# Other instruction durations in the scheduler of a hybrid encoder trunk

## The chip, the cores and the metric

The program runs on one core of a Trainium2 chip. The metric is the device time of one execution in microseconds (us), the median of several runs; less is better. The core has a matrix engine (TensorE, in the rows PE, its weight loads PEld), a vector engine (VectorE, DVE), a scalar engine (ScalarE, ACT), GpSimd (POOL), and a queue (SyncE, SP) from which all transfers of this kernel are issued. Each engine takes its instructions strictly in the order in which the program was written; an instruction whose input isn't there holds up all that stand behind it on its engine.

## The reference

Two layers with shared weights run over two groups of tokens, 512 and 256, of width 1024. Everything is float32. Per layer:

```
h = rmsnorm(x) ; proj = h @ w_in            (q, k, v of four attentions A, B, C, D and 4 x 1024 gates)
o_A: neighbourhood attention with a bias    o_B: grouped-query attention, normed q and k, rotary
o_C: differential attention, ALiBi          o_D: sliding window with a sink, ALiBi
merged = sum over the branches of sigmoid(gate_b) * (o_b @ w_branch_b)
x += rmsnorm(merged @ w_out)
u = rmsnorm(x) @ w_up ; c = conv of width 3 over the tokens ; f = (gelu(gate) * val) @ w_down
x += rmsnorm(f)
```

## The kernel before

Features lie on the 128 partitions and the 768 tokens of both groups side by side on the free axis. Every operand of a product is split into two float32r parts h and l, and a product is made in three passes (h*h, h*l, l*h). So a block of 128 output features with a contraction over 1024 is 8 x 3 x 2 = 48 matmuls, 24 with 512 columns and 24 with 256.

What matters here is how the order of the instructions comes about. The program is written by about a dozen Python generators ("tasks"): the main line of a layer (projections, gates, output projection, feed-forward part), three attention `worker`s, loaders of bias tiles and branch outputs, tasks that empty PSUM, the norms. `Flow` keeps an estimated clock for each engine. Each helper that issues an instruction (`mm`, `tr`, `act`, `_dve` and those that call it, `rsqrt`, `dma`) adds that instruction's estimated duration to its engine's clock and returns the time at which the result may be used, 150 ns (`HOP`) after the estimated end. A task that needs a result says from which time on it can go on. `Flow.run` always resumes the ready task of the highest priority, where "now" is the estimated clock of TensorE; if none is ready, that clock is set forward to the next task's time, which is an estimated idle time of TensorE. Nothing of these times goes onto the chip: only the order of the instructions does.

The main line has the lowest priority, so its matmuls fill TensorE while an attention worker waits for ScalarE or VectorE. What it does meanwhile is a fixed list, `JOBS` (L58): the projections and, as `t`, 19 gate blocks made early (`EARLY`, L60), whose tanh is kept in DRAM. A unit of attention is one head for 256 queries (`unit`, L915): logits, bias and row maximum (L967, for B L949), exp, reciprocal (L994), scaling, transposes (L400), the split of the transposed probabilities, the product with the values, the sum of its two halves. There are 48 units a layer, in the order D, A, B, A, C; three run at a time.

After the last job the main line goes on with `gates` (L1204) for A, B, C, D in turn. Before its products for a branch it needs that branch's output back from DRAM, split (`o_load`, L1140): three times a buffer of the pool `P` (12 buffers, which the attention units also use), a transfer, a copy on ScalarE and a subtraction on VectorE. Then come the output projection and the feed-forward part. Each of the two ends with blocks that are made token group by token group (`grouped_tail`, L697), and as a group is done its norms are started (`sandwich` L637, `pre_norm` L579), while TensorE works on the next group.

All matrix products and the mean squares are issued at L396 in `mm`, transposes at L400, ScalarE's instructions at L412, VectorE's mostly at L426, L430 and L435.

Of the kernel before, what the change touches and what calls it, by code (L numbers as in the profile page):

```python
"""Hybrid gated encoder trunk on one core.

Activations are kept with features on partitions and the tokens of both request groups side by side on the
free axis (prompt 0..511, sample 512..767).  Every float32 operand x of a matrix product is split exactly into
h = float32r(x) and l = x - h, and a product is accumulated as h*h + h*l + l*h (attention logits also carry l*l).
"""
# [11 lines left out]
F32 = mybir.dt.float32  # L18
# [4 lines left out]
PSUM = bass.MemoryType.PSUM  # L23
# [3 lines left out]
KB = DM // 128  # L27
# [8 lines left out]
# the FFN's hidden blocks, in the parts that are on chip together  # L36
THIRDS = ((0, 7), (7, 14), (14, 22))
BR = "ABDC"
# the branches in the order of their gating
# [7 lines left out]
# columns of the per-layer parameter tile  # L47
P_N = 0            # four norm gains, KB columns each
P_GQ = 32          # gqa q gain, gqa q gain of the rotation partner, same for k
P_SUB = 36  # L50
P_LAM = 37         # q1, k1, q2, k2 (32 each), the same on every partition
P_SINK = 165       # four columns, the same on every partition
P_CONV = 169       # per up block: tap 0, tap 1, tap 2, bias
# [3 lines left out]
# What the tensor engine does while the attention runs: projections, and the products of early gates (t).  # L57
JOBS = "V D t A0 t t t VC B A1 t t t t t Cq0 t t Ck0 t t Cq1 Ck1 t t t t t t".split()  # L58
# the gates (branch, block) made early, in order
# [3 lines left out]
def unit_keys():  # L63
    """The weight units of a layer in the order of their use."""
# [26 lines left out]
def unit_data(key, w_in, w_branch, w_out, w_up, w_down):  # L91
    """The unit as [128, n]: contraction rows on partitions, then k block, then output column."""
# [39 lines left out]
def host_arrays(inputs, depth):  # L132
# [31 lines left out]
    # rpb laid out by (column, row offset, key column), NEG outside the column window  # L164
# [8 lines left out]
    # constants of the shapes  # L173
# [30 lines left out]
# blocks of w_out and of the last third of the FFN that are computed token group by token group  # L204
# [4 lines left out]
class Flow:  # L209
    """Emits the instructions of several tasks in an order that follows an estimate of the engines' times.  # L210

    A task is a generator that emits instructions and yields the time before which it has nothing to emit."""
# [34 lines left out]
class Slots:  # L247
    """The buffers of one tag: counts the live ones and knows when a free one may be written."""
# [6 lines left out]
    def ready(self):  # L255
        """The number of buffers that may be written now."""
        return sum(t <= self.flow.now for t in self.freed)
# [18 lines left out]
def both(*needs):  # L276
    """Waits until every one of the (slots, n) is free."""
    while any(s.ready() < n for s, n in needs):
        yield needs[0][0].flow.now + 100
# [21 lines left out]
class Pair:  # L301
    """Weights whose two parts lie in two buffers."""
# [13 lines left out]
class Part:  # L316
    """Weights in the columns of h whose tokens come to be known only after the weights' use."""
# [16 lines left out]
class Block:  # L334
    """A [128, 768] result in PSUM: in a double bank, or with another one in a double bank (their first 512
    columns) and a bank (the rest)."""
# [15 lines left out]
    def parts(self):  # L352
        """Its access patterns, with their columns."""
        if self.full is not None:
            return [(self.full, 0, T)]
        return [(self.half[0], 0, TP), (self.half[1], TP, T)]
# [6 lines left out]
def mixed(a, b):  # L363
    """The elements of a and b, each in its order, evenly mixed, a first."""
    key = [(i / len(x), n, e) for n, x in enumerate((a, b)) for i, e in enumerate(x)]
    return [e for _, _, e in sorted(key)]


class Trunk:
# [23 lines left out]
    def mm(self, out, lhsT, rhs, start, stop, *deps):  # L393
        n = out.shape[-1]
        ns = n * 0.4218 * (4 if lhsT.dtype == F32 else 1)
        self.nc.tensor.matmul(out=out, lhsT=lhsT, rhs=rhs, start=start, stop=stop)  # L396
        return self.f.on("pe", max(ns, 30), *deps)
# [12 lines left out]
    def act(self, out, in_, func, *deps, **k):  # L410
        n = self.size(out)
        self.nc.scalar.activation(out=out, in_=in_, func=func, **k)  # L412
        ns = n * 0.8336 + 80
# [8 lines left out]
    def _dve(self, out, *deps, rate=0.96, fixed=70):  # L422
# [6 lines left out]
    def stt(self, out, a, s, b, op0, op1, *deps):  # L429
        self.nc.vector.scalar_tensor_tensor(out=out, in0=a, scalar=s, in1=b, op0=op0, op1=op1)  # L430
        return self._dve(out, *deps, fixed=130)

    def ts(self, out, a, s1, s2, op0, op1, *deps):
# [4 lines left out]
        return self._dve(out, *deps, rate=1.92, fixed=70 if isinstance(s1, float) else 130)  # L438
# [73 lines left out]
    PASSES = ((0, 0), (0, 1), (1, 0))  # L512

    def mblock(self, out, w, rhs, nk, off=0, wait=None):
        """out: list of (PSUM AP, column range); w: unit; rhs(k, part, c0, c1): moving operand."""
# [16 lines left out]
    def bank(self):  # L532
        """A bank, of a double one or, if that leaves one for the norms, a single one."""
# [4 lines left out]
    def anyblock(self):  # L538
        """As dblock, but in two single banks if they are free sooner."""
# [14 lines left out]
    def rstd_bcast(self, b, n, t):  # L554
        """b: bank with the mean squares of n token tiles in columns 0, 2, ..; leaves 1/sqrt(mean + eps) on
        every partition, one column per token."""
# [10 lines left out]
    def mean_square(self, b, x, first, last, t):  # L567
        """Adds the mean over the partitions (and the middle axis) of x [128, j, 256], which holds squares."""
# [10 lines left out]
    def pre_norm(self, G, x, gain, h, last, first=False):  # L579
        """h = split(rmsnorm(x) * gain) for a group; x: four [128, 2, 256] APs, overwritten,  # L580
        with the times when they are there and when they may be written."""
# [55 lines left out]
    def sandwich(self, G, mix, msq, x_old, x_new, pre, h):  # L637
        """x_new = x_old + rmsnorm(mix) * gain; then h = split(rmsnorm(x_new) * pre) unless it is the end.
        mix comes multiplied by the gain, msq holds the squares without it."""
# [27 lines left out]
    def mix_evac(self, cols, blk, m, groups, mix, msq, gain, acc=None):  # L667
        """Brings an m block of mix (or of the last third of the FFN), times the gain of the norm to come, to
        SBUF and adds its squares."""
# [29 lines left out]
    def grouped_tail(self, tail, nk, key, rhs, wait, mix, msq, gain, sandwich, acc=None):  # L699
        """The first output blocks over all tokens, the others group by group, each group's norms started as it  # L700
        ends."""
# [38 lines left out]
    def v_tiles(self, name, units, tiles, vg):  # L740
        """Values of four heads, tokens on partitions: for each head h and l side by side."""
# [37 lines left out]
    def q_stack(self, src, scale, t0, users):  # L779
        """Two heads' queries, [h; l] for the first and [l; h] for the second."""  # L780
# [11 lines left out]
    def k_stack(self, src, t0, users):  # L792
        """Two heads' keys, for each the parts h and l on both halves of the partitions."""
# [11 lines left out]
    def head_stats(self, src, t):  # L805
        """1/rms over each half of the partitions of src [128, 768], as [128 tokens, 6 tiles, 2 halves]."""
# [12 lines left out]
    def bcast_mul(self, out, a, gain, s, tmp, *deps):  # L819
        """out = a * (1/rms of its half), rms given per token; tmp [128, 768] is overwritten."""  # L820
# [19 lines left out]
    def rope(self, blk, col, cs, key):  # L840
        """Rotated heads of a projection block, before (queries) or after (keys) the rms norm's division."""
# [24 lines left out]
    def c_stack(self, blk, scale, order, users):  # L866
        """32-wide sub-heads of two heads: for each head [128, 2, 768], the parts given by order on four
        quarters of the partitions."""
# [27 lines left out]
    UNITS = (0, 2, 1)  # prompt queries 0..255, sample, prompt queries 256..511  # L896
# [18 lines left out]
    def unit(self, name, h, u, q, k, v, bias, scales=None, oc=None):  # L915
        """Attention of one head for 256 queries (two tiles)."""
# [164 lines left out]
    def worker(self):  # L1081
        """Runs queued attention units, in order, as their operands become ready."""
# [531 lines left out]
```

## Time and profile before

| | |
|---|---|
| median of 3 runs | 2583.24 us (2583.02 to 2583.34) |
| span of the profiled execution, first to last instruction | 2580.6 us |
| TensorE, VectorE, ScalarE busy in it | 2543.3, 1458.1, 1133.5 us |
| mean granted clock of TensorE | 0.996 |

The span is the profiled execution's own time from its first to its last instruction; the device time of the runs is 2.6 us longer. Busy time is the time in which at least one instruction of the engine is shown as running. A matmul is shown for longer than the next one takes to start, so a wait of under some 0.1 to 0.2 us is covered by its tail and isn't shown as idle.

### The profile page before, as it was taken

Reading aid. Unit: us, or ns where it says so; the run is one execution under the profiler, and the core shown is the slowest. Engines: PE = TensorE matmul, PEld = TensorE weight load, DVE = VectorE, ACT = ScalarE, POOL = GpSimd, SP = SyncE. Lnnn points to the kernel's source line nnn. Section 1 sums busy time; section 2 is a strip of 40 time slices with the busy share of each in tenths; the row PEclk is TensorE's granted clock in tenths of the full one; section 3 lists DMA queues with packets and bytes.
Section 4 is the critical chain, followed back from the end, with each engine's and each line's share of the span. In section 5 each row is a group of like instructions: output and inputs, shape, how many; then the busy total and the mean of one; then the engine's idle time right before and its main releaser. Section 6 shows DMA issues by size and latency. Waiting matters only on the chain.

```text
span 2580.6 us, 39698 instructions
## 1 busy us (share of the span) xinstructions
PE 2543.3 (99%) x15964; PEld 2281.7 (88%) x15964; DVE 1458.1 (57%) x2766; ACT 1133.5 (44%) x2166; POOL 39.8 (2%) x38
## 2 busy tenths in 40 slices
PE   7999999999999999999999999999999999999998
PEld 7898888888998888888998988888889988888888
DVE  5567667746475335345566665775565752453554
ACT  5465666522463323233545556654225532331342
POOL 0001000000000000000000000000000000000000
PEclk9999999999999999999999999999999999999999
DMA  3333244433331111111333333443423212112122
GB/s 130 108 116 104 90 145 132 134 134 102 111 103 62 61 66 59 65 66 58 123 96 99 107 109 112 134 135 121 159 70 129 91 54 70 65 52 72 58 82 82
DMA packets 113576, 249.43 MB, mean 97 GB/s; under 512 B 13168, under 2 KB 56816, under 8 KB 113392
## 3 DMA queue, kind: packets, MB, share of 16 engines
q1 hardware_dynamic: 113392, 246.90, 29.7%
q8 instruction: 125, 2.05, 0.3%
q14 instruction: 59, 0.48, 0.1%
HBM read 194.15 MB, written 33.82 MB: 88 GB/s over the span
## 4 chain that ended last, share of the span: by engine, by line
PE 95%; DVE 3%; ACT 1%; issue 1%; DMA 0%; SPq 0%; POOLq 0%; DVEq 0%; ACTq 0%
PE d L396 78%; PE b L396 14%; PE b L400 3%; DVE g L426 1%; DVE p L426 1%; ACT p L412 1%; ACT g L412 0%; DVE h L426 0%; DVE w L426 0%; DVE p L967 0%; ACT w L412 0%; DMA par<-par 0%; ACT h L412 0%; DVE p L430 0%; SPq L445 0%
## 5 line engine op out<-in xcount | busy, mean ns | idle before, releaser
L396 PE MATMUL d<-h,w 128*128 128x512 f32 (+1 forms) x7248 | 1328.2, 338 | 0.0
L396 PEld LDWEIGHTS d<-h,w 128*128 128x128 f32 x7248 | 1106.4, 189 | 148.5
L426 DVE TENSOR_TENSOR w<-raw,w 128x1024 fp32r<-128x1024 f32 (+1 forms) x216 | 260.5, 1208 | 282.2 <-ACT w L412 271.2
L396 PE MATMUL d<-g,w 128*128 128x256 f32 (+1 forms) x2196 | 376.4, 329 | 1.6 <-ACT g L412 1.5
L430 DVE SCALAR_TENSOR_TENSOR p<-d,par,p 128x511 f32<-128x511 f32 (+1 forms) x328 | 204.3, 623 | 292.1 <-ACT p L412 286.3
L396 PEld LDWEIGHTS d<-g,w 128*128 128x128 f32 x2196 | 324.0, 189 | 43.3 <-ACT g L412 2.1
L412 ACT ACTIVATE p<-d,par 128x512 f32<-128x512 f32 (+1 forms) x164 | 111.1, 677 | 384.9 <-PE d L396 255.3
L412 ACT ACTIVATE w<-raw 128x1024 fp32r<-128x1024 f32 (+1 forms) x216 | 224.0, 1039 | 116.7 <-PE d L396 105.6
L412 ACT ACTIVATE p<-p,st 128x512 f32<-128x512 f32 (+2 forms) x288 | 178.1, 629 | 121.1 <-DVE st L994 67.9
L412 ACT ACTIVATE g<-d 128x128 fp32r<-128x128 f32 (+3 forms) x136 | 77.8, 574 | 284.7 <-PE d L396 247.9
L396 PE MATMUL d<-h,bi 128*128 128x256 f32 (+1 forms) x912 | 160.0, 334 | 0.0
L396 PEld LDWEIGHTS d<-h,bi 128*128 128x128 f32 x912 | 137.1, 189 | 19.1
L426 DVE TENSOR_TENSOR p<-b,p 128x512 fp32r<-128x512 f32 (+1 forms) x160 | 103.2, 658 | 63.1 <-ACT p L412 62.5
L412 ACT ACTIVATE p<-b 128x512 fp32r<-128x512 f32 (+1 forms) x160 | 90.6, 574 | 96.4 <-PE b L400 95.5
L396 PE MATMUL b<-g,g 128*128 128x512 f32 (+2 forms) x384 | 107.6, 356 | 2.7 <-DVE p L426 1.8
L396 PE MATMUL d<-g,bi 128*128 128x512 f32 (+1 forms) x636 | 107.7, 326 | 0.0
L396 PEld LDWEIGHTS d<-g,bi 128*128 128x128 f32 x636 | 93.0, 189 | 11.1
L396 PE MATMUL d<-w,h 128*128 128x256 f32 x672 | 93.7, 296 | 8.2 <-ACT h L412 3.4
L396 PE MATMUL b<-p,g 128*128 128x256 f32 x608 | 99.1, 287 | 1.1 <-DVE p L426 1.1
L412 ACT ACTIVATE g<-p 128x512 fp32r<-128x512 f32 x112 | 56.5, 540 | 98.1 <-DVE p L426 64.5
L967 DVE CUSTOM_DVE_ANT_0 p<-b,bi 128x512 f32<-128x512 f32 (+1 forms) x144 | 85.9, 597 | 22.5 <-PE b L396 18.1
L396 PEld LDWEIGHTS d<-w,h 128*128 128x128 f32 x672 | 88.3, 202 | 10.7 <-ACT h L412 4.0
(104 smaller groups left out, 2454.1 us busy)
## 6 DMA issues: line engine op xcount, KB each, us to landing
raw<-weights SPq DMA_DIRECT2D x236, 512.0 KB, 3.6
raw<-weights SPq DMA_DIRECT2D x32, 448.0 KB, 3.3
g<-g SPq DMA_DIRECT2D x128, 96.0 KB, 2.2
x<-g SPq DMA_DIRECT2D x36, 256.0 KB, 2.1
p<-x SPq DMA_DIRECT2D x36, 256.0 KB, 4.1
bi<-na_bias SPq DMA_DIRECT2D x64, 128.0 KB, 2.8
p<-x_in SPq DMA_DIRECT2D x24, 256.0 KB, 5.3
g<-g SPq DMA_DIRECT2D x16, 384.0 KB, 3.6
```

The source lines that it names most:

```text
L396: self.nc.tensor.matmul(out=out, lhsT=lhsT, rhs=rhs, start=start, stop=stop)
L400: self.nc.tensor.transpose(out=out, in_=in_, identity=self.ident)
L412: self.nc.scalar.activation(out=out, in_=in_, func=func, **k)
L426: self.nc.vector.tensor_tensor(out=out, in0=a, in1=b, op=op)
L430: self.nc.vector.scalar_tensor_tensor(out=out, in0=a, scalar=s, in1=b, op0=op0, op1=op1)
L967: nc.vector.tensor_tensor_reduce(out=p[:, :nkey], in0=s[:, :nkey], in1=bt, scale=1.0, scalar=init, op0=ALU.add, op1=ALU.max, accum_out=mx[ ...
```

## The change

Five constants of the scheduler's estimates are replaced. A matmul is counted at 0.457 instead of 0.4218 ns a column and at least at 109 instead of 30 ns. An instruction of ScalarE keeps 0.8336 ns an element and gets a fixed part of 190 instead of 80 ns. One of VectorE keeps its rate and gets a fixed part of 155 instead of 70 ns; scalar_tensor_tensor and tensor_scalar get 215 instead of 130 ns where their scalar lies in memory. The estimates of transposes, GpSimd, transfers and of the hop between engines stay. No computation, buffer, queue or list is touched; the same instructions are issued, in an order that the new estimates give. (The diff also empties comments and docstrings; the line numbers stay.)

```
     def mm(self, out, lhsT, rhs, start, stop, *deps):
         n = out.shape[-1]
-        ns = n * 0.4218 * (4 if lhsT.dtype == F32 else 1)
+        ns = n * 0.457 * (4 if lhsT.dtype == F32 else 1)
         self.nc.tensor.matmul(out=out, lhsT=lhsT, rhs=rhs, start=start, stop=stop)
-        return self.f.on("pe", max(ns, 30), *deps)
+        return self.f.on("pe", max(ns, 109), *deps)
...
     def act(self, out, in_, func, *deps, **k):
         n = self.size(out)
         self.nc.scalar.activation(out=out, in_=in_, func=func, **k)
-        ns = n * 0.8336 + 80
+        ns = n * 0.8336 + 190
         for a, x in (("scale", 92), ("bias", 143), ("accum_out", 93)):
...
-    def _dve(self, out, *deps, rate=0.96, fixed=70):
+    def _dve(self, out, *deps, rate=0.96, fixed=155):
         return self.f.on("dve", self.size(out) / rate + fixed, *deps)
...
     def stt(self, out, a, s, b, op0, op1, *deps):
         self.nc.vector.scalar_tensor_tensor(out=out, in0=a, scalar=s, in1=b, op0=op0, op1=op1)
-        return self._dve(out, *deps, fixed=130)
+        return self._dve(out, *deps, fixed=155 if isinstance(s, float) else 215)
...
-        return self._dve(out, *deps, rate=1.92, fixed=70 if isinstance(s1, float) else 130)
+        return self._dve(out, *deps, rate=1.92, fixed=155 if isinstance(s1, float) else 215)
```

## Rows read from the trace of the kernel before

**Rows 1.** The page: span, and busy time, share and instructions of each engine.

```profile
span 2580.6 us, 39698 instructions
...
PE 2543.3 (99%) x15964; PEld 2281.7 (88%) x15964; DVE 1458.1 (57%) x2766; ACT 1133.5 (44%) x2166; POOL 39.8 (2%) x38
```

**Rows 2.** Windows of 25 us: stretch, busy us of each engine, clock, DMA.

```profile
0.00:25.00 25.00, 11.31 (x58) 10.04 (x59) 13.16 (x21) 16.83 (x31) 1.61 (x6) 1.00 0.66 223
...
1300.00:1325.00 25.00, 22.18 (x169) 21.23 (x168) 19.22 (x42) 16.17 (x42) 2.06 (x3) 0.93 0.18 62
...
2550.00:2575.00 25.00, 19.77 (x161) 19.02 (x159) 13.78 (x30) 6.38 (x14) 1.39 (x2) 0.93 0.28 95
```

**Rows 3.** Windows by stage of the first layer: attention's tail, gates, feed-forward part.

```profile
471.00:514.00 43.00, 41.70 (x255) 36.04 (x254) 28.59 (x63) 22.49 (x44) 2.27 (x1) 1.00 0.32 108
514.00:640.00 126.00, 126.00 (x729) 111.12 (x728) 70.98 (x81) 29.88 (x39) 0.00 (x0) 1.00 0.36 121
...
750.00:1225.00 475.00, 475.00 (x2722) 413.55 (x2721) 225.69 (x328) 161.06 (x243) 0.00 (x0) 1.00 0.19 64
```

**Rows 4.** The chain that ended last, in order of time: start, us, what.

```profile
770.27 449.45 PE d L396 x2544
```

**Rows 5.** Groups by line and shape: count, busy us, mean ns of one, idle before.

```profile
L426 DVE TENSOR_TENSOR p<-b,p 128x512 fp32r<-128x512 f32 x144 | 96.7, 686 | 56.1 <-ACT p L412 55.5
...
L412 ACT ACTIVATE p<-b 128x512 fp32r<-128x512 f32 x144 | 84.6, 596 | 85.3 <-PE b L400 84.4
```

**Rows 6.** Timeline of ScalarE at the boundary of the layers: instructions that follow each other directly.

```profile
1299.70 0.26 ACT L412 ACTIVATE g<-d 128x128 fp32r<-128x128 f32 x1
...
1301.32 3.30 ACT L412 ACTIVATE g<-g,par 128x256 f32<-128x256 f32 x8
```

**Rows 7.** Timeline of VectorE in the same stretch.

```profile
1299.99 0.29 DVE L426 TENSOR_TENSOR g<-d,g 128x128 fp32r<-128x128 f32 x1 [0.28 <-ACT g L412]
...
1303.23 2.48 DVE L426 TENSOR_TENSOR g<-g,b 128x512 f32<-128x512 f32 x4 [1.35 <-ACT g L412]
```

**Rows 8.** Timeline of TensorE: two waits during the jobs, with what follows.

```profile
159.24 0.98 PE L396 MATMUL d<-w,h 128*128 128x256 f32 x6 [0.76 <-ACT p L412]
...
419.05 0.50 PE L396 MATMUL b<-g,g 128*128 128x512 f32 x1 [0.47 <-DVE p L426]
419.38 1.57 PE L396 MATMUL d<-h,w 128*128 128x512 f32 x8
```

**Rows 9.** The stretch between the last job's and branch A's products, as a window.

```profile
471.19:480.03 8.84, 7.54 (x46) 5.73 (x45) 6.85 (x23) 7.12 (x17) 0.00 (x0) 1.00 0.24 79
```

**Rows 10.** Groups of TensorE's instructions in that stretch.

```profile
L396 PE MATMUL b<-p,g 128*128 128x256 f32 x20 | 3.6, 303 | 0.6 <-DVE p L426 0.6
L400 PE MATMUL b<-const,p 128*128 128x128 f32 x16 | 2.1, 272 | 0.0
L396 PE MATMUL b<-g,g 128*128 128x512 f32 x4 | 2.0, 492 | 0.7 <-DVE p L426 0.4 <-DVE st L967 0.3
```

**Rows 11.** Timeline of SP's queue: the loads of branch A's output, and B's third.

```profile
461.02 0.38 SPq L445 DMA_DIRECT2D p<-oA  x1
...
472.20 0.37 SPq L445 DMA_DIRECT2D p<-oA  x1
...
513.12 0.44 SPq L445 DMA_DIRECT2D p<-oB  x1
```

**Rows 12.** Timelines of VectorE and ScalarE: B's first row maximum, the last unit's sum.

```profile
235.38 0.69 DVE L949 TENSOR_REDUCE st<-b 128x1 f32<-128x512 f32 x1
...
502.07 0.38 ACT L412 ACTIVATE s<-b 64x256 f32<-64x256 f32 x1 [1.41 <-PE b L396]
```

**Rows 13.** Timeline of TensorE at the boundary of the layers.

```profile
1316.59 1.02 PE L396 MATMUL b<-const,p 128*128 128x2 f32 x8 [0.99 <-DVE p L426]
1317.47 1.92 PE L396 MATMUL d<-w,h 128*128 128x256 f32 x12
...
1324.65 2.65 PE L396 MATMUL d<-w,h 128*128 128x256 f32 x14 [1.06 <-DVE h L426]
```

More of the change, by code (lines that the diff above doesn't have):

```diff
@@ L394, in mm @@
         n = out.shape[-1]
-        ns = n * 0.4218 * (4 if lhsT.dtype == F32 else 1)
+        ns = n * 0.457 * (4 if lhsT.dtype == F32 else 1)
         self.nc.tensor.matmul(out=out, lhsT=lhsT, rhs=rhs, start=start, stop=stop)
-        return self.f.on("pe", max(ns, 30), *deps)
+        return self.f.on("pe", max(ns, 109), *deps)
     def tr(self, out, in_, *deps):
@@ L412, in act @@
         self.nc.scalar.activation(out=out, in_=in_, func=func, **k)
-        ns = n * 0.8336 + 80
+        ns = n * 0.8336 + 190
         for a, x in (("scale", 92), ("bias", 143), ("accum_out", 93)):
@@ L420, in copy, with _dve @@
         return self.act(out, in_, AF.Copy, *deps, scale=scale)
-    def _dve(self, out, *deps, rate=0.96, fixed=70):
+    def _dve(self, out, *deps, rate=0.96, fixed=155):
         return self.f.on("dve", self.size(out) / rate + fixed, *deps)
@@ L430, in stt @@
         self.nc.vector.scalar_tensor_tensor(out=out, in0=a, scalar=s, in1=b, op0=op0, op1=op1)
-        return self._dve(out, *deps, fixed=130)
+        return self._dve(out, *deps, fixed=155 if isinstance(s, float) else 215)
     def ts(self, out, a, s1, s2, op0, op1, *deps):
@@ L437, in ts @@
             self.nc.vector.tensor_scalar(out=out, in0=a, scalar1=s1, scalar2=s2, op0=op0, op1=op1)
-        return self._dve(out, *deps, rate=1.92, fixed=70 if isinstance(s1, float) else 130)
+        return self._dve(out, *deps, rate=1.92, fixed=155 if isinstance(s1, float) else 215)
     def rsqrt(self, out, in_, n, *deps):
```

## The prediction

> **What bounds the kernel.** I read the page first. TensorE is busy for 2543.3 of 2580.6 us [rows 1], so the whole idle time is 37.3 us, and no other engine comes near it (VectorE 57%). The change alters neither the number nor the shapes of the instructions, so TensorE's work is the same after it; only the idle time and what it is made of can move. The next view is the windows. Of the 37.3 us, 13.7 lie in the first 25 us [rows 2], before and while the first group is normed: the first inputs and the first norms set that, with nothing to put in their place. At the end 5.2 us from 2550 to 2575 [rows 2] and the 5.6 after it are the last norms, behind which no product is left. The gates and the whole feed-forward part show none: 126.00 of 126.00 and 475.00 of 475.00 us busy [rows 3]. What order can touch is the remaining 12.8 us, less the end of the first norms: two waits of 0.76 and 0.47 us in a layer's attention [rows 8], 1.30 in its tail from 471 to 514 us [rows 3], and 2.82 at the boundary of the layers [rows 2], which is 2 x 2.5 + 2.8 = 7.9 us, since the second layer repeats the first; with what the tail hides (below), about 11, or 0.4%. What order can lose has no such bound. The reader should see in these rows a kernel in which almost every wait of an engine is hidden behind a matrix product that doesn't depend on it, and ask of the new estimates whether that product still stands there.
>
> **The change part by part.** *TensorE's estimate.* In the feed-forward part 2544 matmuls, half of 512 and half of 256 columns, took 449.45 us [rows 4]: 449.45 / (1272 x 768) = 0.460 ns a column. The old 0.4218 was 8% short, the new 0.457 is right within 1%. The floor of 109 ns holds for a few hundred 2-column matmuls and matters little.
>
> *ScalarE's and VectorE's estimates.* The new ones are the mean durations that the trace gives: 533 + 155 = 688 ns for a VectorE operation on 512 columns, against 686 shown; 427 + 190 = 617 for a ScalarE copy, against 596 [rows 5]. But the scheduler uses an estimate twice: as the time for which the engine is taken, and, plus 150 ns, as the time until a consumer may start. The timelines show what each of these is. Taken: eight ScalarE instructions of 256 columns with a scale from memory ran in 3.30 us, 0.41 each [rows 6]; the old estimate is 213 + 80 + 92 = 385 ns, the new 495. Four VectorE operations of 512 columns ran in 2.48 us, 0.62 each [rows 7]; old 603, new 688. So the durations shown overlap, and back to back the old numbers were nearly right. Until the consumer: ScalarE's instruction of 1299.70 ended at 1299.96 and VectorE's, which waited for it, began at 1299.99 [rows 6, 7], 0.03 us later, not 0.15. A VectorE operation of 512 columns is thus worth 686 + 30 = 716 ns to its consumer; the old model says 603 + 150 = 753, the new 838. The old numbers were 5% too long here and the new ones are 17%. The change makes one estimate better (TensorE) and two worse.
>
> The Trainium skill speaks to the second point: its page "Perfetto Trace Analysis", section "Optimizing Scalar/DVE Operations", gives about 60 ns (VectorE) and 93 ns (ScalarE) of fixed engine time on SBUF and says that the profiled latency is about twice this, because the write's acknowledgement overlaps with the next instruction. By that rule the durations of a trace aren't what an engine is taken for, and this change puts a latency where an occupancy belongs. The overlapped rows just read agree with it. By the page's 60 ns the new fixed part of VectorE is 95 ns too long, by the rows at least 68; it changes no term below.
>
> *What this does to the order.* For the order only the ratio to TensorE's clock counts, since TensorE's clock is the scheduler's "now". Take one unit of branch A with 512 keys from its last logits on. VectorE: row maximum, its negation, reciprocal, two splits of 512 columns, the final sum, six steps of +85 ns; ScalarE: exp, scaling, two copies of 512 columns, one of 256, five of +110. From the constants these eleven steps add up to 4.94 us before and 6.00 after. TensorE's steps in it go from 1.74 to 1.81 us (eight transposes stay), and 15 hops of 150 ns stay. Together 8.92 to 10.06 us, +12.7%, while the filler beside it is counted 0.457 / 0.4218 = +8.3% longer. So a unit takes 1.127 / 1.083 = 4% more filler than before. From branch B on the three workers set the pace, from the first row maximum at 235.38 to the last unit's sum at 502.07 [rows 12]: 267 us, of which 4% is 10.7 us. The list of jobs is fixed. So attention ends about 10 us later against the filler, and the rest of it lies beside the gates.
>
> *What that costs.* During the jobs nothing: the more time a unit is given, the surer its input is there when TensorE comes to it. In the two waits of [rows 8] other products followed directly; if the more cautious order removes them, -1.23 a layer, -2.5 in all. At the boundary of the layers a mean square stood 0.99 us before its input with 12 free products right behind [rows 13]: -1.0. In the tail the cover is thinner. The main line has to have A's output back before it can multiply it; its three loads were issued between 461.02 and 472.20 us [rows 11], as buffers came free, and from 471.19 to 480.03 there was attention alone. In these 8.84 us TensorE had 46 matmuls [rows 9]: with 0.460 ns a column and 109 ns a transpose, 25 of 256, 16 transposes and 5 of 512 columns [rows 10] (the last two stand singly) come to 5.9 us, so 3.0 us or 34% were lost, though only 1.30 are shown idle. A tail that is 10.7 us longer costs nothing if all of it lies beside gate products (lower bound) and 10.7 x 0.34 = 3.6 us a layer if all of it falls into such a stretch (upper bound). The gate stage has products enough [rows 3], but attention units go before the load in taking buffers. I take the middle, 1.8 a layer, +3.6.
>
> Sum: -2.5 - 1.0 + 3.6 = +0.1 us. On the span of 2580.6 that is 2580.7, and with the 2.6 us between span and median 2583.3.
>
> **The rivals.** *The tail of the attention decides, slower.* Place: 471 to 525 us and the same in the second layer. At its upper bound the sum is -3.5 + 7.2 = +3.7; if besides the loads for branch B, whose third was issued at 513.12 [rows 11], wait for attention's buffers and the main line stands a second time as long as it did at A (3.0 us a layer), +9.7: 2593. For it: three workers hold the pool and come first. Against it: a gate block of B needs no output and covers 24 x 768 columns, 8.5 us. It decides from 5.2 us on, which is 15 us of attention alone over both layers at 34%.
>
> *The norms decide, slower.* At each group's norm the copies, squares and corrections follow each other with some 19 VectorE operations of 512 columns, each counted about 70 to 90 ns too long: 1.3 to 1.7 us, and ScalarE's eight at 83 more, 0.7. So the products that use a normed group are put some 2.2 us late behind filler; at the three boundaries where products follow, if the filler is then gone, +6.6: 2590. Against it: the queues run as soon as inputs come, and filler put ahead of a product isn't lost as long as it had to be done.
>
> *More waits go than I count, faster.* If all that order can give back goes, -11: 2572; half to three quarters of it and no loss in the tail, -5.5 to -8: about 2576. For it: a more cautious estimate leaves TensorE more often with a ready instruction, and TensorE's own is now right. Against it: the largest part, the tail, has no filler to take.
>
> *The change does nothing.* If the ratios (4%) were too small to turn the order, 2583.2. I count that with the forecast; with some 40 thousand instructions the order will change, but the time needn't.
>
> **How the numbers follow.** About 0.2%, 5.2 us, is what can be told from no change. Forecast, terms that cancel: 0.50, its own range 2578 to 2588. Tail slower 0.20, norms slower 0.10; faster 0.20. So faster 0.20, same 0.50, slower 0.30. The range that leaves out a tenth on each side reaches halfway into the faster case and to just beyond the slower ones: 2575 to 2595.
>
> **What would show it.** Right: TensorE's busy time within a few us of 2543, and the idle time again in the first norms, the tail and the boundary; the last unit's sum some 10 us of filler later; the waits at 159 and 419 us gone; the stretch without main-line products before A's first product as long as now or longer by up to a third. Wrong: an idle stretch in the gates or the feed-forward part, which have none now; attention that ends earlier; a boundary between layers with over 5 us idle; a change of TensorE's clock in the attention.

## The result, and the profile after

The change made the kernel slower: 2629.64 us median (2628.57 to 2631.13), against 2583.26 for before in the same comparison, a ratio of 1.0181 [1.0167, 1.0196]. The forecast of 2583.3 with its range of 2575 to 2595 was wrong, and so were the two slower rivals at 2590 and 2593.

The page of after, its first lines, which answer to [rows 1]:

```profile
span 2626.8 us, 39672 instructions
...
PE 2563.4 (98%) x15964; PEld 2297.1 (87%) x15964; DVE 1458.2 (56%) x2766; ACT 1134.0 (43%) x2172; POOL 40.3 (2%) x38
```

The span grew by 46.2 us. TensorE's idle time went from 37.3 to 63.4 us, only 26.1 more; the other 20.1 us are TensorE's busy time, for the same 15964 matmuls. So waits have gone where idle time doesn't show them. ScalarE has six instructions more (2172 against 2166): a gate's block that finds no double bank of PSUM free takes two single ones (`anyblock`), and six times its tanh is then made in two parts.

The chain that ended last, of after, gives two marks that stand at the same work in both kernels, the starts of the longest run of matmuls in each of the two feed-forward parts (start us, us, what):

```profile
789.58 449.45 PE d L396 x2544
...
2092.60 449.45 PE d L396 x2544
```

The same view of before, second layer (the first is [rows 4]):

```profile
2046.20 449.45 PE d L396 x2544
```

The 449.45 us themselves have not changed. Up to the first mark 19.3 us were lost (789.58 - 770.27), between the marks 27.1, after the second -0.2. All of it lies in attention, output projection and the boundary of the layers. Windows of after in the first layer and at the boundary:

```profile
200.00:225.00 25.00, 20.34 (x126) 17.59 (x124) 15.05 (x32) 11.08 (x20) 2.27 (x1) 0.97 0.34 95
225.00:250.00 25.00, 23.26 (x122) 20.52 (x123) 18.00 (x38) 13.25 (x25) 2.27 (x1) 0.82 0.20 50
475.00:500.00 25.00, 22.44 (x114) 18.30 (x115) 23.42 (x66) 15.97 (x39) 2.27 (x1) 0.86 0.15 50
725.00:750.00 25.00, 22.26 (x175) 22.08 (x174) 17.15 (x30) 13.84 (x30) 1.44 (x2) 0.93 0.45 147
...
1300.00:1325.00 25.00, 23.69 (x191) 23.49 (x190) 14.99 (x32) 13.18 (x29) 2.06 (x3) 0.95 0.39 127
1325.00:1350.00 25.00, 18.87 (x143) 17.96 (x143) 18.95 (x39) 13.98 (x34) 0.70 (x1) 0.91 0.13 44
```

Before, the first two of these windows were busy throughout, at full clock:

```profile
200.00:225.00 25.00, 25.00 (x168) 22.73 (x167) 21.97 (x42) 12.28 (x21) 4.54 (x2) 1.00 0.34 99
225.00:250.00 25.00, 25.00 (x148) 21.89 (x147) 14.30 (x27) 13.90 (x25) 0.00 (x0) 1.00 0.41 107
```

The first two rows of after are the surprise: a standstill in the middle of the jobs, with the granted clock down to 0.82 behind it.

To size such places without trusting "busy", I use the count that the prediction made for its tail: each matmul at 0.460 ns a column and at least 109 ns, summed by shapes; what is left of a stretch is lost time. Groups of TensorE's instructions of after, 200 to 250 us:

```profile
L396 PE MATMUL d<-h,w 128*128 128x512 f32 x74 | 28.8, 424 | 0.0
L396 PE MATMUL d<-h,w 128*128 128x256 f32 x74 | 21.6, 292 | 0.0
L396 PE MATMUL b<-p,g 128*128 128x256 f32 x34 | 6.2, 304 | 1.4 <-DVE p L426 1.4
L396 PE MATMUL b<-const,g 128*128 128x2 f32 x24 | 4.1, 298 | 2.4 <-DVE s L426 2.4
L400 PE MATMUL b<-const,p 128*128 128x128 f32 x26 | 4.1, 275 | 2.4 <-DVE st L967 2.4
L396 PE MATMUL b<-g,g 128*128 128x512 f32 x12 | 3.9, 402 | 0.0
L396 PE MATMUL b<-g,g 128*128 128x256 f32 x4 | 1.1, 375 | 0.2 <-DVE st L967 0.2
```

86 of 512 columns, 112 of 256 and 50 small ones cost 20.3 + 13.2 + 5.4 = 38.9 of 50 us: 11.1 lost, of which idle time shows 6.4. The same count on before's instructions in that stretch gives 50.6 of 50, so it is good to about 0.6 us; small negative values below are this error. Done on all kernels, it gives this table (lost us, both layers added, except the boundary):

| kernel | time, us | B, 190-260 and 1490-1560 | A's tail, 440-550 and 1740-1850 | output norms, 700-770 and 2000-2090 | boundary, 1300-1360 | C, 260-440 and 1560-1740 |
|---|---|---|---|---|---|---|
| before | 2583.3 | -1.4 | 4.3 | 1.3 | 7.0 | 0.3 |
| after | 2629.6 | 21.2 | 16.8 | 12.6 | 12.9 | 0.1 |
| pe_only | 2607.6 | 0.7 | 14.3 | 6.1 | 7.0 | 5.0 |
| actdve_only | 2648.2 | 27.5 | 23.4 | 4.0 | 10.3 | 8.4 |
| act_only | 2640.4 | 21.0 | 12.4 | 4.1 | 12.9 | 10.9 |
| dve_only | 2617.0 | 21.7 | 19.9 | 3.4 | 10.5 | -1.9 |
| split | 2601.4 | -0.9 | 13.7 | 3.4 | 8.3 | 2.6 |
| nudge | 2596.9 | -0.8 | 19.2 | 1.4 | 6.7 | 2.1 |
| hop30 | 2609.4 | -1.2 | 18.2 | 7.8 | 7.4 | 8.8 |
| jobs_later | 2627.8 | -1.1 | 30.4 | 14.0 | 10.2 | 4.3 |
| jobs_more | 2618.9 | -1.0 | 13.4 | 13.4 | 12.4 | -0.2 |
| fetch_before | 2577.0 | -1.5 | -1.7 | 1.0 | 7.1 | 0.0 |
| fetch_after | 2629.1 | 20.3 | 10.1 | 12.6 | 10.8 | 0.1 |
| fetch_later | 2615.6 | -1.2 | 14.0 | 13.4 | 12.5 | 3.8 |
| fetch_nudge | 2582.9 | -0.8 | 1.3 | 1.3 | 6.9 | 1.9 |
| fetch_split | 2592.2 | -1.1 | 1.7 | 3.6 | 7.2 | 3.3 |
| fetch_pe | 2590.3 | 0.9 | -1.6 | 4.9 | 7.2 | 5.8 |
| fetch_hop30 | 2595.4 | -1.2 | -1.2 | 8.3 | 6.3 | 10.6 |

For after against before that is +22.6 at branch B, +12.5 in A's tail, +11.3 at the output norms and +5.9 at the boundary. The stretches outside the table lost 6.2 us less than before, 2.3 of these before 190 us. Together, with -0.2 at C, 45.9 of the span's 46.2.

What happens at B? TensorE's waits there, from the timeline of after:

```profile
213.15 4.42 PE L396 MATMUL d<-h,w 128*128 128x512 f32 x24
...
221.53 0.66 PE L400 MATMUL b<-const,p 128*128 128x128 f32 x4 [2.35 <-DVE st L967]
...
225.33 2.69 PE L396 MATMUL b<-const,g 128*128 128x2 f32 x12 [2.41 <-DVE s L426]
228.05 1.65 PE L396 MATMUL d<-h,w 128*128 128x512 f32 x4
```

From 217.57 to 228.05 there is no product of the main line at all. Counted in blocks of 48 matmuls, the block that ends at 217.57 isn't one of B's three but the next in the list, A's second query projection (`A1`), and the one that starts at 228.05 is the key projection behind it. VectorE's timeline says what is late, after first, then before:

```profile
223.74 1.00 DVE L846 STREAM_SHUFFLE g<-d 128x768 f32<-128x768 f32 x1
...
225.21 0.95 DVE L430 SCALAR_TENSOR_TENSOR g<-d,g 64x768 fp32r<-64x768 f32 x1
227.03 0.96 DVE L430 SCALAR_TENSOR_TENSOR g<-d,g 64x768 fp32r<-64x768 f32 x1 [0.87 <-ACT g L412]
```

```profile
217.17 1.02 DVE L846 STREAM_SHUFFLE g<-d 128x768 f32<-128x768 f32 x1
```

The shuffle belongs to the rotary part on B's third block. That block was complete at 207.55 after and at 216.28 before, so it lay for 16.2 us instead of 0.9. The two instructions of L430 read A's query block (`q_stack`, L779), and 0.06 us after the second of them, at 228.05, the main line goes on. In the code both readers begin by taking one of the 13 buffers of the pool `G`, and the main line itself stands in `q_stack` until it has one. Ahead of B's jobs the 13 are spoken for: six hold values, four the queries and keys of D, three those of A's first heads. D's come back only as its units are done with them, and D's last units are late: the sum of the 12th unit, after, then before.

```profile
204.68 0.38 ACT L412 ACTIVATE s<-b 64x256 f32<-64x256 f32 x1 [4.01 <-PE b L396]
```

```profile
182.00 0.38 ACT L412 ACTIVATE s<-b 64x256 f32<-64x256 f32 x1
```

D's first row maximum, after, then before (timeline of VectorE):

```profile
82.28 0.62 DVE L967 CUSTOM_DVE_ANT_0 p<-b,bi,par 128x384 f32<-128x384 f32 x1
```

```profile
83.69 0.62 DVE L967 CUSTOM_DVE_ANT_0 p<-b,bi,par 128x384 f32<-128x384 f32 x1
```

From it to the 12th sum the units took 204.68 - 82.28 = 122.4 us; before it was 182.00 - 83.69 = 98.3, so +25%. It isn't spread evenly: the sixth sum came at 138.59 against 138.31, the seventh at 155.16 against 143.47. One of the places where it comes from, TensorE's timeline of after:

```profile
141.22 6.41 PE L396 MATMUL d<-h,w 128*128 128x512 f32 x36
147.46 0.60 PE L400 MATMUL b<-const,p 128*128 128x128 f32 x4
```

VectorE took the reciprocals of two units at 144.64 and 145.36 and had scaled their rows by 145.91; their transposes stand behind 36 matmuls of an early gate. This one place cost them some 2 us, so most of the lag has other places, which aren't shown one by one. A run of 28 stands in before's order too (146.41).

The other places, TensorE's timeline of after. A mean square in the norms of the output projection, and the products that use a normed group at the boundary:

```profile
744.69 1.07 PE L396 MATMUL b<-const,p 128*128 128x2 f32 x8 [2.74 <-DVE p L426]
...
1347.55 0.58 PE L396 MATMUL d<-w,h 128*128 128x256 f32 x1 [3.96 <-ACT h L412]
1349.22 1.01 PE L396 MATMUL d<-w,h 128*128 128x256 f32 x3 [1.09 <-DVE h L426]
```

B's first row maximum, which [rows 12] has at 235.38:

```profile
254.78 0.69 DVE L949 TENSOR_REDUCE st<-b 128x1 f32<-128x512 f32 x1 [0.91 <-PE b L396]
```

The loads of A's output on SP's queue, 466.13 to some 476 against 461.02 to 472.20 in [rows 11], and the last unit's sum, 31.1 us later than in [rows 12]:

```profile
466.13 0.38 SPq L445 DMA_DIRECT2D p<-oA  x1
473.19 3.50 SPq L445 DMA_DIRECT2D p<-oA  x2
```

```profile
533.20 0.38 ACT L412 ACTIVATE s<-b 64x256 f32<-64x256 f32 x1 [3.79 <-PE b L396]
```

### The profile page after: what moved, and what is told of

It is laid out like the page before. It is cut to its first block, busy times and chain, and to the rows that moved or that the text cites. A ratio compares the mean times of both kernels' runs of the same rounds, so it can differ in the third digit from the quotient of the medians.

```text
span 2626.8 us, 39672 instructions
## 1 busy us (share of the span) xinstructions
PE 2563.4 (98%) x15964; PEld 2297.1 (87%) x15964; DVE 1458.2 (56%) x2766; ACT 1134.0 (43%) x2172; POOL 40.3 (2%) x38
## 4 chain that ended last, share of the span: by engine, by line
PE 93%; DVE 4%; ACT 2%; issue 1%; DMA 0%; SPq 0%; POOLq 0%; DVEq 0%; ACTq 0%
PE d L396 74%; PE b L396 16%; PE b L400 3%; DVE g L426 1%; ACT p L412 1%; ACT g L412 1%; DVE p L426 1%; DVE h L426 1%; DVE p L967 1%; DMA g<-g 0%; DVE p L430 0%; DMA par<-par 0%; ACT w L412 0%; DVE w L426 0%; DVE st L435 0%
## 5 line engine op out<-in xcount | busy, mean ns | idle before, releaser
L396 PE MATMUL d<-h,w 128*128 128x512 f32 (+1 forms) x7008 | 1291.0, 339 | 0.5 <-DVE g L430 0.5
L396 PEld LDWEIGHTS d<-h,w 128*128 128x128 f32 x7008 | 1075.7, 190 | 145.3 <-DVE g L430 0.9
L396 PE MATMUL d<-g,w 128*128 128x512 f32 (+1 forms) x2136 | 373.3, 332 | 1.6 <-ACT g L412 1.5
L430 DVE SCALAR_TENSOR_TENSOR p<-d,par,p 128x511 f32<-128x511 f32 (+1 forms) x328 | 204.4, 623 | 291.4 <-ACT p L412 285.6
L412 ACT ACTIVATE p<-p,st 128x256 f32<-128x256 f32 (+2 forms) x288 | 178.5, 629 | 153.3 <-DVE st L994 77.7
L396 PE MATMUL d<-h,bi 128*128 128x512 f32 (+1 forms) x864 | 150.5, 334 | 0.0
L396 PEld LDWEIGHTS d<-h,bi 128*128 128x128 f32 x864 | 129.5, 189 | 17.9
L396 PE MATMUL b<-h,w 128*128 128x256 f32 (+1 forms) x816 | 140.2, 329 | 0.0
L396 PEld LDWEIGHTS b<-h,w 128*128 128x128 f32 x816 | 120.2, 189 | 14.0
L396 PE MATMUL d<-g,bi 128*128 128x256 f32 (+1 forms) x696 | 115.4, 322 | 0.0
L396 PEld LDWEIGHTS d<-g,bi 128*128 128x128 f32 x696 | 100.4, 189 | 10.9
```

## The experiments

All are the kernel before or after with constants, the two lists or the start of one load altered. Edits are shown against after, unless said otherwise. Each ratio is to before on the same chip.

**Which estimate does it.** First each half of the change.

pe_only, TensorE's new estimate alone:

```
-        ns = n * 0.8336 + 190
+        ns = n * 0.8336 + 80
-    def _dve(self, out, *deps, rate=0.96, fixed=155):
+    def _dve(self, out, *deps, rate=0.96, fixed=70):
...
```

> Only TensorE's estimates are new (0.457 ns a column, floor 109); ScalarE's and VectorE's are the old ones. Theory (the longer ScalarE and VectorE estimates put attention late against the filler): here the ratio goes the other way, a unit's chain is counted about 8.99 instead of 8.92 us while filler is 8.3% longer, so attention runs ahead of where it ran before; no idle stretch at branch B's rotary part (200 to 250 us), 2575 to 2592 us. Rival 1 (TensorE's estimate did the damage): 2610 us or more, idle at branch B. Rival 2 (any other order is worse than this one, whatever the constants): 2595 to 2630.

Measured 2607.57, ratio 1.0094 [1.0077, 1.0111]. Rival 2's range holds it. Attention isn't late here (12th unit 169.00, last sum 496.87), B costs nothing, and still 24 us are lost. That the estimate which is now within 1% costs 24 us by itself fells my division into one good and two bad estimates.

actdve_only, the other half:

```
-        ns = n * 0.457 * (4 if lhsT.dtype == F32 else 1)
+        ns = n * 0.4218 * (4 if lhsT.dtype == F32 else 1)
-        return self.f.on("pe", max(ns, 109), *deps)
+        return self.f.on("pe", max(ns, 30), *deps)
```

> Only ScalarE's and VectorE's estimates are new; TensorE's are the old ones. Theory: the chain of a unit is counted 12% longer and the filler not at all, three times the shift of the whole change, so attention is later still: 2635 to 2680 us, idle stretches at branch B and in the tail longer than in the changed kernel. Rival 1 (TensorE's estimate): about 2583. Rival 2 (any other order): 2595 to 2630, no larger than the whole change.

Measured 2648.20, ratio 1.0253 [1.0238, 1.0269], as the theory has it: without the longer filler estimate attention falls back further (12th unit 216.61, last sum 556.88) and B costs 27.5.

act_only and dve_only split it once more. Both have TensorE's old numbers, as above. In act_only VectorE's are old too, so ScalarE's 190 alone is new:

```
-    def _dve(self, out, *deps, rate=0.96, fixed=155):
+    def _dve(self, out, *deps, rate=0.96, fixed=70):
```

> The kernel before with ScalarE's fixed part alone new, 190 instead of 80 ns. Theory of pace: five steps of 110 ns, +6% for a unit's chain, half of what both engines' estimates do: 2600 to 2630 us, with attention later than before and waits at branch B or in the tail. Rival (any reshuffle costs the same): as the nudge.

Measured 2640.37, ratio 1.0222 [1.0207, 1.0237]; above the theory's range. In dve_only ScalarE's is old, and VectorE's 155 and 215 alone are new:

```
-        ns = n * 0.8336 + 190
+        ns = n * 0.8336 + 80
```

> The kernel before with VectorE's fixed parts alone new, 155 and 215 instead of 70 and 130 ns. Theory of pace: six steps of 85 ns, +6%, and the engine that is taken longest in the attention: 2605 to 2635 us, at least as much as ScalarE's alone. Rival (any reshuffle costs the same): as the nudge.

Measured 2617.04, ratio 1.0130 [1.0113, 1.0147]; in the range, but ScalarE's constant alone costs more than VectorE's, which I had not expected. The parts don't add up (24 + 57 + 34 for a whole of 46): an order isn't a sum of its causes. What holds in the four kernels up to here with B's loss (after, actdve_only, act_only, dve_only) is that the 12th unit ends after 200 us (204.68, 216.61, 212.57, 205.98), and that the main line pauses at the same place, between the query and the key projection of `A1`, for 10.5, 11.9, 9.9 and 6.2 us. In the five with B at its old place where the unit ends by 182.40 (before, and pe_only, split, nudge, hop30) none is lost at B, and the key projection follows at once.

**Is it B's place?** jobs_later moves two of the gate jobs ahead of B:

```
-JOBS = "V D t A0 t t t VC B A1 t t t t t Cq0 ...
+JOBS = "V D t A0 t t t VC t t B A1 t t t Cq0 ...
```

> The changed kernel with two of the early gates moved from behind A's second projections to ahead of branch B's (same work, same number of jobs). Theory with its mechanism (at branch B the main line and the rotary tasks wait for buffers of the pool of 13 that late attention units still hold): two gate blocks, some 17 us of TensorE's work and more with attention beside it, give the units time to let go; the idle at 200 to 250 us, 6.4 us shown, goes, and about 11 us a layer are won: 2603 to 2615 us. Rival (the loss there is the rotary chain's own length or order, not a want of buffers): the idle moves with branch B and stays, 2622 to 2640.

Measured 2627.81, ratio 1.0176 [1.0161, 1.0192]: the time is in the rival's range, but the rival's idle stretch isn't there, B's loss is gone. Windows of jobs_later:

```profile
200.00:225.00 25.00, 25.00 (x159) 22.36 (x157) 18.75 (x45) 12.64 (x25) 2.27 (x1) 1.00 0.30 89
225.00:250.00 25.00, 25.00 (x158) 22.30 (x158) 20.68 (x37) 12.74 (x22) 4.54 (x2) 1.00 0.24 62
450.00:475.00 25.00, 22.20 (x110) 17.09 (x109) 15.93 (x45) 14.49 (x32) 0.00 (x0) 0.89 0.37 124
```

The filler put ahead of B was missing at the end of the jobs: A's tail went from 16.8 to 30.4 us. So B's loss is cured by delaying B and `A1`, as the want of buffers has it, and nearly all of the 22 us comes back elsewhere. jobs_more adds two gate blocks to the early ones instead of moving any:

```
+JOBS = "V D t A0 t t t VC t t B A1 t t t t t Cq0 ...
-EARLY = [... "... A2 C4 A3".split()]
+EARLY = [... "... A2 C4 A3 D5 D6".split()]
```

> The changed kernel with two more gate blocks of branch D (D5, D6) made early, ahead of branch B's projections; they are taken from the gate stage, so TensorE's work is the same. Moving two blocks there from the end took away the waits at branch B and gave them back in the tail; here nothing is taken from the end. Theory: the waits at branch B go (about 11 us a layer) and the tail stays as in the changed kernel: 2605 to 2615 us. Rival (attention's end, later by the two blocks, exposes the tail as before): 2622 to 2630.

Measured 2618.90, ratio 1.0138 [1.0123, 1.0153]: 10.7 less than after, 4 short of the theory. B costs nothing and A's tail 13.4, but the gates (550-700 and 1850-2000) lost 14.5 us more than in after: D's, now shorter, have waits that before hadn't (timeline of jobs_more):

```profile
663.63 0.61 PE L396 MATMUL d<-g,w 128*128 128x512 f32 x2 [1.83 <-ACT g L412]
```

**Occupancy or latency?** The estimate of an instruction serves as both. hop30 keeps all new durations and cuts the hop added for the consumer from 150 to the 30 ns that [rows 6, 7] show, so the latencies are nearly right and the occupancies remain too long (by [rows 6, 7] 495 against 410 ns and 688 against 620, 21% and 11%, not the 15 to 24% below). The hop is one number for all engines, so the handovers from TensorE, GpSimd and the transfers, which no row here gives, are cut with it:

```
-    HOP = 150
+    HOP = 30
```

> The changed kernel with a hop of 30 instead of 150 ns, as the handover in the rows: the time until a consumer may start is then right (688 + 30 = 718 ns), and the time for which ScalarE and VectorE are taken is still 15 to 24% too long. A unit's chain is counted 6.00 + 1.81 + 0.45 = 8.26 us, less than before the change. Theory A (the chain's latency sets attention's pace): attention ahead of where it was before the change, no waits at branch B: 2588 to 2610 us. Theory B (the time taken sets it, since three units and the filler's splits share the two engines): waits at branch B stay, 2618 or more.

Measured 2609.36, ratio 1.0106 [1.0093, 1.0120], in theory A's range. The 12th unit is back at its old time (timeline of ScalarE), and B stands no more (windows):

```profile
182.40 0.68 ACT L412 ACTIVATE s<-b 64x256 f32<-64x256 f32 x2
```

```profile
200.00:225.00 25.00, 25.00 (x163) 22.64 (x162) 20.71 (x39) 12.23 (x20) 3.12 (x2) 1.00 0.30 83
225.00:250.00 25.00, 25.00 (x152) 22.09 (x152) 17.09 (x30) 13.92 (x24) 2.27 (x1) 1.00 0.39 103
475.00:500.00 25.00, 19.57 (x111) 16.02 (x109) 16.17 (x33) 13.53 (x26) 0.00 (x0) 0.93 0.28 85
```

Boundary and output norms improve too (12.9 to 7.4, 12.6 to 7.8). So a shorter time to the consumer is enough to have attention back on time, with the occupancies as long as ever. But A's tail (third row) and C still lose.

split gives TensorE its shown rate, the others their old (occupancy) numbers, and the hop what makes the sum the shown latency:

```
-    HOP = 150
+    HOP = 120
...
-        ns = n * 0.8336 + 190
+        ns = n * 0.8336 + 80
...
```

> TensorE's new estimates, ScalarE's and VectorE's old ones, and a hop of 120 instead of 150 ns: occupancy and time to the consumer both near what the rows show (603 + 120 = 723 ns against 716). Theory: like TensorE's estimates alone, attention a little earlier still: 2572 to 2592. Rival (a cautious hop is what keeps TensorE from waiting): several us slower than with TensorE's alone, 2595 or more.

Measured 2601.36, ratio 1.0072 [1.0057, 1.0087]: the rival. With each estimate set to what the rows show, as well as this model can hold it, the kernel is still 19 us slower than before.

**Is any other order worse?** nudge is the kernel before with one constant 2% higher:

```
-        ns = n * 0.4218 * ...
+        ns = n * 0.4300 * ...
```

> The kernel before with one estimate moved a little: TensorE 0.430 instead of 0.4218 ns a column, 1.9%, a quarter of the change; the floor stays at 30 ns. Theory of pace (the loss grows with how far attention is moved against the fixed list of jobs): a quarter of what TensorE's estimates cost alone, 2583 to 2592 us. Rival (the old order is a special one, and any reshuffle costs about the same): 2595 to 2612.

Measured 2596.88, ratio 1.0051 [1.0036, 1.0066]; the rival again. Nearly the whole loss is one place, A's tail (4.3 to 19.2). Timelines of nudge, TensorE and SP's queue, and a window from the last job's end to A's first product:

```profile
479.98 1.94 PE L400 MATMUL b<-const,p 128*128 128x128 f32 x8 [4.23 <-DVE p L430]
```

```profile
458.47 0.37 SPq L445 DMA_DIRECT2D p<-oA  x1
...
467.08 0.39 SPq L445 DMA_DIRECT2D p<-oA  x1
...
478.07 0.37 SPq L445 DMA_DIRECT2D p<-oA  x1
```

```profile
475.55:483.70 8.15, 3.08 (x13) 1.99 (x13) 7.87 (x24) 6.88 (x16) 0.00 (x0) 0.81 0.11 32
```

The third load is issued 11.0 us after the second; for 9.2 of these the queue waits for an instruction of an attention unit on VectorE (L430), which frees a buffer. The main line has no product for TensorE till that load is there and split. Before had its three loads within 11.2 us [rows 11], nudge in 19.6. But the stretch without a product of the main line is no longer here (8.15 us) than before (8.84 [rows 9]). What differs is the cover: attention had matmuls of 5.9 us for TensorE in it before, and here 12 transposes, 1.3 us by the same count.

**Is it the late fetch?** The fetch_ kernels start the load of A's output two jobs before the end of the list, instead of after it:

```
         for n, job in enumerate(JOBS):
+            if n == len(JOBS) - 2:
+                self.o_box["A"] = box = []
+                self.f.start(self.o_load("A", box), 1)
             if n == 1:
```

> The kernel before (old estimates), with the load of branch A's output started two jobs earlier, ahead of the last two early gates instead of behind them. Theory (TensorE's loss between the last job and A's products is the wait for that load's third buffer and split): the loss there, some 3 us a layer, goes: 2574 to 2581 us. Rival (any reshuffle of this order costs 10 us or more): 2590 to 2605.

Measured 2576.96, ratio 0.9977 [0.9968, 0.9985]: faster than both kernels, as the theory has it. A's loads are issued from 436.08 on and the tail loses nothing. Window of fetch_before; [rows 3] had 1.30 idle in 471 to 514:

```profile
475.00:500.00 25.00, 25.00 (x154) 22.13 (x153) 19.44 (x43) 12.45 (x26) 0.00 (x0) 1.00 0.31 99
```

> The changed kernel with the same early load of A's output. Theory: of the 9 us a layer that the tail now loses the part at A's products goes, the waits at branch B and in the norms stay: 2610 to 2622 us. Rival (the load only takes its buffers from the attention units, which then end later): 2626 or more.

Measured 2629.05, ratio 1.0179 [1.0165, 1.0193]: no gain. A's tail lost 6.7 us less; the stretches 550-700 and 1850-2000 lost 4.8 more, in the first layer without a wait that shows, and the feed-forward parts 7.7 more. There, at 1245 and 1248 us and the same in the second layer, products wait 0.76 and 1.85 us for their operand (`g`), where after waits 0.74 in all; what makes that operand late isn't shown.

> The changed kernel with both remedies: two early gates moved ahead of branch B's projections, and A's load two jobs earlier. Theory: waits at branch B gone (11 us a layer) and the tail, where that move gave them back, covered at A's products (9 us a layer): 2600 to 2614 us. Rival (what is lost is a fixed sum that only changes its place): 2622 to 2632.

On jobs_later it gave 2615.63, ratio 1.0129 [1.0114, 1.0145]: 12.2 less than jobs_later, 1.6 above the theory's range.

The remaining four ask it of the orders in which attention isn't late.

> The scheduler of before with TensorE at 0.430 ns a column (2596.9 us), and branch A's output fetched two jobs earlier. Theory: what such an order loses, it loses where the main line stands without A's output; I read 7 and 8 us there in the two layers, so the time falls by 10 to 17 us, to 2580 to 2587. Rival: the loss is that of any order other than the one that the list of jobs was written for, and goes elsewhere if it is taken away here: 2592 or more.

2582.87, ratio 0.9999 [0.9990, 1.0009], 14.0 less: theory.

> TensorE's new estimate, ScalarE's and VectorE's old ones, a hop of 120 ns (2601.4 us), and A's output fetched two jobs earlier. Theory (the missing output of A): 6.2 and 7.8 us fall away, 2585 to 2591. Rival (the loss goes elsewhere): 2597 or more.

2592.20, ratio 1.0034 [1.0021, 1.0048], 9.2 less: between the two, 1 us from the theory. The tail lost 12.0 less, the gates behind it 2.6 more.

> TensorE's new estimate alone (2607.6 us), and A's output fetched two jobs earlier. Theory (the missing output of A): 7.3 and 8.3 us fall away, but branch C's late operands still make the jobs end 9 us later: 2590 to 2597. Rival (the loss goes elsewhere): 2603 or more.

2590.34, ratio 1.0028 [1.0019, 1.0038], 17.2 less: theory.

> All new durations with a hop of 30 ns (2609.4 us), and A's output fetched two jobs earlier. Theory (the missing output of A): 6.9 and 8.1 us fall away, 2592 to 2599. Rival (the loss goes elsewhere): 2605 or more.

2595.36, ratio 1.0047 [1.0032, 1.0062], 14.0 less: theory. In all four the table's column of A's tail falls to between -1.6 and 1.7. So the fetch is the common loss of the orders that don't stand at B. What fetch_hop30 still loses against before is 10.3 us at C, 7.0 at the output norms and 4.8 in the gates, net of gains in A's tail and at the boundary.

## Why the prediction was wrong

**TensorE's bound** held: only the order's waits could move, the feed-forward parts stayed at 449.45 us. "What order can lose has no such bound" was right, and was then not carried into the range.

**The step that failed** is "What that costs. During the jobs nothing: the more time a unit is given, the surer its input is there when TensorE comes to it." This holds for TensorE's own wait on that unit; of the two waits in [rows 8] the first went, and what lies before 190 us lost 2.3 us less; for the second there is another at 428.07, of 0.68. It doesn't hold for what the units keep others from. The jobs after D need what its units are done with: A's second query projection ends at 217.57 and can't be taken out of PSUM for want of a buffer, and for 10.5 us TensorE gets nothing from the main line. That cost 22.6 us over both layers, half of the whole. Shown is that the standstill goes with a 12th unit after 200 us, that it ends when the block is read (227.99, and 228.05 the next product), and that it goes away when these jobs stand later or attention earlier. That the block waits for one of the 13 buffers of `G` follows from the code; a run with another number of buffers is not among the experiments.

**The 4%** was worked out from branch B on, and there it was of the right size: from B's first row maximum to the last sum after took 533.20 - 254.78 = 278.4 us against 266.7, of which 5.6 are the tail's own loss in this layer, so some 6 us where the prediction said 10.7. What it left out is D, whose 12 units took 25% longer. A change of 4% in a ratio isn't spread evenly: D's first six units took 1.7 us longer than before, the next six 22.4.

**The tail** was the rival that named the right place and mechanism (A's loads wait for attention's buffers), priced at up to 3.6 us a layer, and 3.0 more if the loads for B stood too. Without the early fetch it costs 6 to 12 a layer in nearly every order tried, 15 in jobs_later. The mis-sized term is the 34%: it was the cover that attention happened to give in one order, taken for a rate. In nudge the same stretch loses 84% (6.8 of 8.15 us).

**The norms** were a rival at +6.6 in three places. They cost +11.3 at the output and +5.9 at the boundary. That hop30 takes back 10.3 of this 17.2 supports its mechanism, a latency counted too long, but no run changes the norms' instructions alone; TensorE's estimate alone also costs 4.8 at the output, which the rival didn't have.

**Occupancy against latency.** The prediction used the Trainium skill, "Perfetto Trace Analysis", section "Optimizing Scalar/DVE Operations": the profiled latency is about twice the fixed engine time, the rest overlapping the next instruction. The overlap was there in [rows 7] (0.62 us each back to back against 0.686 shown). The section's 60 ns are for operands in SBUF; the operations of [rows 7] read PSUM (`b`) as well, so the prediction's 95 ns don't apply to them, and the rows' 68 stand. The engines' occupancy was the smaller part of the price, as far as two orders can be compared: hop30, with the occupancies still too long, has attention back on time, and split, which also sets them right, is only 8 us faster (2601.4 against 2609.4). The second half of the same double count, 150 ns of hop on a duration that already holds the latency, was by this the more expensive one.

**Its own signs** worked: "a boundary between layers with over 5 us idle" (7.4 from 1300 to 1350) and "a change of TensorE's clock in the attention" (0.82 from 225 to 250) were named as what would show it wrong.

## What to carry to other kernels

With a fixed list of jobs, correcting the estimated durations gives a new order and not by itself a better one. Here each of seven other sets of constants, one of them a 2% nudge, was 0.5 to 2.5% slower. Price such a change by asking at each place where the main line needs something back (a PSUM block, a buffer, a fetched output) how much independent work stands behind it, and what happens if the holder is 20 us late; that a consumer's input is surer to be there says nothing of those. And repair the thin place in the program, not the estimates: two jobs' notice for one fetch took 9 to 17 us from the four orders in which attention was on time and 6 from the old one, though nothing from the change's own order, in which attention is late.

## What the runs showed of the hardware

A standstill costs more than its idle time, because of the granted clock. Windows of 5 us of after at B:

```profile
220.00:225.00 5.00, 1.16 (x6) 0.72 (x6) 3.70 (x10) 2.68 (x5) 0.00 (x0) 0.85 0.28 85
225.00:230.00 5.00, 4.65 (x19) 4.40 (x20) 4.03 (x9) 2.22 (x4) 0.54 (x1) 0.50 0.07 16
230.00:235.00 5.00, 5.00 (x22) 4.39 (x22) 4.31 (x12) 2.58 (x5) 1.73 (x1) 0.62 0.00 0
235.00:240.00 5.00, 5.00 (x33) 4.49 (x33) 3.69 (x6) 3.08 (x7) 0.00 (x0) 1.00 0.34 105
```

After a stretch with 1.16 of 5 us busy the clock is at its lower level, 1.2 GHz (0.50), for most of ten microseconds in which TensorE is 4.65 and 5.00 of 5 us busy. Twelve matmuls of 2 columns at 225.33 took 2.69 us; before, at 207.16 and the full clock, 1.39. By these rows the clock withheld up to (0.15 + 0.50 + 0.38) x 5 = 5.2 us of full-speed time, which with the 6.4 us of idle time accounts for the 11.1 lost there. The page's busy time counts the slow part as work. The same holds for the whole: the mean granted clock of the profiled execution was 0.989 after and 0.996 before, so by estimate 0.011 x 2626.8 = 29 us were withheld against 0.004 x 2580.6 = 10. That is some 19 us more, close to the 20.1 us by which TensorE's busy time grew.
